# Encoder layer on one core: value projections computed token by token, a first stage without GpSimd arithmetic, merge transfers issued by GpSimd, scores two steps at a time

## The chip, the core and the metric

One core of a Trainium2 chip runs the whole program. The time is the device time of one execution in microseconds (us); less is better. Its engines each work through a queue of their own, in order: TensorE (PE; its weight loads are shown as PEld), VectorE (DVE), ScalarE (ACT), GpSimd (POOL), and SyncE (SP), which here only issues transfers. An instruction that waits holds up everything behind it in its engine's queue.

## The reference, cut to what matters

One layer of an encoder on 512 tokens of 1024 features, all float32:

```python
h = layer_norm(x, ln0_g, ln0_b)
proj = h @ w_in[l] + b_in[l]
y_a = (gate_b * dwconv3(gate_c * hin, conv_w[l])) @ w_a[l]
for g, (window, dil) in enumerate(((128, 1), (512, 4), (2048, 16))):
    o, lse = dilated_window_attention(q[:, :, g], k[:, :, g], v[:, :, g], dil, window // (2 * dil), slopes[g])
wts = jax.nn.softmax(jnp.stack(lses, 0), axis=0)
comb = jnp.sum(wts[..., None] * jnp.stack(outs, 0), axis=0)
mix = (g_a * y_a + g_b * (comb @ w_b[l])) @ w_o[l] + b_o[l]
h = layer_norm(ALPHA * h + mix, ln1_g[l], ln1_b[l])
f = gelu(dwconv3(a, ffn_conv_w[l]) + ffn_conv_b[l]) * gte      # a, gte: halves of h @ w_up + b_up
h = layer_norm(ALPHA * h + f @ w_down[l] + b_down[l], ln2_g[l], ln2_b[l])
```

There are three groups of 8 heads, 64 wide. The three groups' outputs of one head slot are added with weights that come from their softmax denominators: this is the "merge" below.

## The kernel before

**Number format.** Every matrix product is done three times with rounded operands: each operand is split into a high part and the rest (`hi` and `lo`), and `mm3` (L312) adds hi·hi, hi·lo and lo·hi. Weights come from memory as chunks of 128 x 2048 numbers (`load`, SP's queue), ACT copies the high part (L261) and DVE subtracts it from the raw chunk (L263). For the first two chunks POOL does the subtraction (`eng` in `split`). `raw`, `hi` and `lo` have rings of 2, 3 and 3 chunks.

**Units.** A unit is 128 columns of the input projection for all 512 tokens: 8 steps of the contraction, 24 products of 128x512, one half of a chunk. The result is feature-major (features on partitions). `in_units` lists them: for each of four head pairs p and each group g a q, a k and a v unit (36), then 24 for the convolution branch.

**First stage.** Token tiles x0 to x3 are loaded, normalised on DVE (L277 to L304), transposed on PE (L345), scaled on ACT and split into `hT` (`feature_major`, L308 to L310), first for x0 and x1 and then for x2 and x3. For each half of the tokens the first four units are computed with 256 columns. Forty products on zeros (`WARM`, L229) come ahead of it.

**Attention.** After each unit `slot` (L597) hands out a little attention work: `transpose_v` (L402) turns a v unit into token-major tiles (four PE transposes, an ACT copy, a DVE subtraction); `Job.a` computes scores of 128 or 256 queries and their exponentials (two jobs a slot for g = 0, one otherwise); `merge` (L525) sends the maxima and sums of group 0 through device memory to bring them into the order of groups 1 and 2 (L529 out, L533 in), computes the weights on DVE and ACT, and sends those of group 0 back (L550 out, L552 in). All four transfers are issued from ACT's queue. From three slots later `Job.b` (L474) scales the exponentials, `b2` (L479 to L482) transposes them, and `c` multiplies with the values; one job a slot each.

After attention follow the convolution's projection, the gates, the output projection, a layer norm, the MLP (L713 on) and the last layer norm.

The order on each engine is that of a scheduler, which starts from the program's order and moves instructions of one engine past each other; `keep_in_program_order` and `issue_after` bind it.

Of the kernel before, what the change touches and what calls it, by code (L numbers as in the profile page):

```python
# [11 lines left out]
P = 128  # L12
# [10 lines left out]
WARM = 40  # L23
# [24 lines left out]
def in_units():  # L48

    units = []  # L50
    for p in range(NPAIR):
        for g in range(3):
            for kind, base in (("q", BLK_Q), ("k", BLK_K), ("v", BLK_V)):
                units.append((kind, p, g, base + g * 4 + p))
    for j in range(8):
        units += [("C", j, 0, BLK_C + j), ("H", j, 0, BLK_H + j), ("B", j, 0, BLK_B + j)]
    return units


def chunk_plan():  # L60

    out = [("in", i, 2048) for i in range(0, len(in_units()), 2)]
# [16 lines left out]
def lay_out_weights(w):  # L79
# [10 lines left out]
    for name, key, cols in chunk_plan():  # L90
        if name == "in":
            c = [block(w_in, units[key + i][3] * P, P) for i in range(2)]
        elif name == "wa":
# [53 lines left out]
def build(tc, x, wst, colt, dist, rows, out):  # L147
# [3 lines left out]
    with ExitStack() as ctx:  # L151
        pool = lambda name, bufs=1, **k: ctx.enter_context(tc.tile_pool(name=name, bufs=bufs, **k))
        const = pool("const")
        wraw = pool("wraw", 2)
        whl = pool("whl", 3)
        blkp = pool("blk", 25)
# [43 lines left out]
        def first_raw(i, c):  # L200
            if i not in raws:
                raws[i] = wraw.tile([P, 2048], F32, tag="raw", name=f"raw{i}")
            src = wst[i * P * 2048 : (i + 1) * P * 2048].rearrange("(p c) -> p c", p=P)
            first_load(raws[i][:, c : c + 1024], src[:, c : c + 1024])
# [20 lines left out]
        for t in kbd:  # L225
            nc.vector.memset(f(t), 0.0)
# [14 lines left out]
        def load(i):  # L241
# [3 lines left out]
            t = wraw.tile([P, 2048], F32, tag="raw", name=f"raw{i}")  # L245
            src = wst[int(offs[i]) : int(offs[i + 1])].rearrange("(p c) -> p c", p=P)
            nc.sync.dma_start(out=t[:, :n], in_=src)
            raws[i] = t

        def split(i):  # L250
# [5 lines left out]
            lo = whl.tile([P, 2048], F32R, tag="lo", name=f"lo{i}")  # L256
            step = 512 if i == 0 else 1024
            starts = (0, 1024, 512, 1536) if i == 0 else range(0, n, step)
            for c in starts:
                part = slice(c, min(c + step, n))  # L260
                nc.scalar.activation(hi[:, part], raws[i][:, part], AF.Copy)  # L261
                eng = nc.gpsimd if i < 2 else nc.vector
                eng.tensor_tensor(lo[:, part], raws[i][:, part], f(hi[:, part]), op=ALU.subtract)  # L263
            splits[i] = (hi, lo)
# [10 lines left out]

        def bn_half(st, z, h):
            nc.vector.bn_stats(out=st[:, h, :], in_=z[:, h * 512 : (h + 1) * 512])  # L277
# [25 lines left out]
        def normalise(z, mean, rstd):  # L303
            nc.vector.tensor_scalar(z, z, mean, rstd, op0=ALU.subtract, op1=ALU.mult)  # L304

        def feature_major(pst, dst, kt, cg, cb, c0, c1):
            t = f32t("lnT")[:, : c1 - c0]
            nc.scalar.activation(t, pst, AF.Identity, bias=col(cb + kt), scale=col(cg + kt))  # L308
            nc.vector.tensor_copy(dst[:, 0, c0:c1], t)
            nc.vector.tensor_tensor(dst[:, 1, c0:c1], t, f(dst[:, 0, c0:c1]), op=ALU.subtract)  # L310
# [16 lines left out]
        first = []  # L327
        for hf in range(2):
# [5 lines left out]
            stats0 += ln_finish(st, f"l0{hf}")  # L334
            for r in rr:
                normalise(xt[r], *stats0[r])
            if hf == 0:
                with tc.issue_after(roots[0]):
                    chunk("in", 0)
            for k0 in range(0, KT, 2):  # L340
                pst = ps(("pt", "s")[k0 // 2 % 2])
# [4 lines left out]
                for k in (k0, k0 + 1):  # L346
                    c = (k % 2) * 256
                    feature_major(pst[:, c : c + 256], hT[k], k, C_G0, C_B0, hf * 256, hf * 256 + 256)
            if hf == 0:
                first = [ps("acc"), ps("acc"), ps("u"), ps("u")]  # L350
            t = slice(hf * 256, hf * 256 + 256)
            for n0, nk in ((0, [(n, k) for k in range(KT) for n in range(2)]), (2, [(n, k) for n in range(2) for k in range(KT)])):
                w = chunk("in", n0)
                for n, k in nk:
                    a = slice(n * 1024 + k * P, n * 1024 + (k + 1) * P)
                    mm3(first[n0 + n][:, t], w[0][:, a], w[1][:, a], hT[k][:, 0, t], hT[k][:, 1, t], k == 0, k == KT - 1)
# [55 lines left out]

        class Job:
# [6 lines left out]
            def a(self):  # L420
                p, g, n = self.key
                q = qk[p, g]
                if (p, g) not in sts:
                    sts[p, g] = small.tile([P, 2, 4, 2], F32, tag="st", name=f"st{p}{g}", bufs=8)
# [60 lines left out]
            def c(self):  # L485

                p, g, n = self.key
                v = vv[p, g]
# [11 lines left out]
                else:  # L500
                    for i in range(2):
                        j, cc = 2 * n + i, slice(i * 256, (i + 1) * 256)
                        mm3(u[:, cc], v[:, 0, j], v[:, 1, j], hi[:, cc], lo[:, cc], g == 1 and i == 0, g == 2 and i == 1)
# [21 lines left out]
        def merge(p):  # L525
# [7 lines left out]
            nc.scalar.dma_start(out=st0.rearrange("p a b c -> p (a b c)"), in_=s1.rearrange("(i r) s -> i (r s)", r=4))  # L533
# [16 lines left out]
            nc.scalar.dma_start(out=s2.rearrange("(i r) h -> i (r h)", r=4), in_=w[:, 7].rearrange("p a b -> p (a b)"))  # L550
            c0 = small.tile([P, 4, 2], F32, tag="c0", name=f"c0{p}", bufs=2)
            nc.scalar.dma_start(out=c0, in_=s2.rearrange("(b p) h -> p b h", p=P))  # L552
# [42 lines left out]
        wait = [0]  # L595

        def slot():  # L597
# [9 lines left out]
            if sums and sums[0].key[0] in cs and wait[0] == 0:  # L607
# [3 lines left out]
            if scores:  # L611
                for _ in range(2 if scores[0].key[1] == 0 else 1):
# [3 lines left out]
                if not any(x.key[0] == p for x in scores) and jb.key[1] == 2:  # L616
                    merge(p)
                    wait[0] = 3
                    order = [(0, 0), (0, 1), (0, 2), (0, 3), (1, 0), (2, 0), (1, 1), (2, 1)]
                    sums.extend(alljobs[(p,) + o] for o in order)  # L620
            wait[0] = max(0, wait[0] - 1)
            scores.extend(late)
            late.clear()

        alljobs = {}
        for n, (kind, a0, a1, blkno) in enumerate(in_units()):
# [6 lines left out]
            slot()  # L633
            if kind in "qkv":
# [7 lines left out]
            else:  # L642
                evac_conv(kind, a0, blkno, o)
# [202 lines left out]
```

## Time and profile before

| what | us |
|---|---|
| median of 3 runs | 988.76 |
| lowest and highest run | 987.72, 989.27 |
| the profiled execution | 988.83 |
| span from its first to its last instruction | 986.7 |
| busy in the span: PE, DVE, ACT, POOL | 968.7, 541.6, 398.2, 42.6 |

The profiled execution stands 0.07 us from the median; 2.1 us of it lie outside the span. Rows name an engine, a line of the kernel, an operation, its output and its inputs (buffer numbers left out), how many instructions the row joins, and their times. The end of a matmul in these rows is modelled, so that neighbouring matmuls overlap in them and "busy" is not the rate of PE; the rate is read from how many start in a stretch.

### The profile page before, as it was taken

What the parts mean: (1) busy time and instruction counts of PE and PEld (TensorE: products, weight loads), DVE (VectorE), ACT (ScalarE), POOL (GpSimd) and SP (SyncE); (2) the same over time, 40 slices, a digit from 0 to 9 for tenths busy, and PEclk for the clock granted to TensorE, in tenths of its full rate; (3) what the DMA queues carried; (4) which work ended last, traced back from release to release, by engine and by line L of the source; (5) the groups of instructions that cost most, each with busy time, mean ns of one, the idle gap of its engine ahead of it and who ended that gap; (6) DMA issues with size and microseconds to landing.
All of it is one profiled execution on the core that took longest, in us unless ns stands there. A gap on an engine that the chain in (4) does not pass through costs nothing.

```text
span 986.7 us, 11756 instructions
## 1 busy us (share of the span) xinstructions
PE 968.7 (98%) x4729; PEld 817.0 (83%) x4729; DVE 541.6 (55%) x874; ACT 398.2 (40%) x679; POOL 42.6 (4%) x150
## 2 busy tenths in 40 slices
PE   7999999999999999999999999999999999999996
PEld 6988888888888888888888888988888888888885
DVE  7856757568565554421344757668443254454256
ACT  4655555555543333322343324544441134443220
POOL 4000000000000000000000000010000000000000
PEclk8999999999999999999999999999999999999998
DMA  6322321222222222225234321242322323222402
GB/s 232 129 87 86 87 86 44 86 86 86 44 86 86 86 86 86 86 86 205 93 107 133 122 88 43 102 176 86 128 75 75 128 88 126 86 86 84 151 4 83
DMA packets 23462, 96.74 MB, mean 98 GB/s; under 512 B 9200, under 2 KB 9584, under 8 KB 13680
## 3 DMA queue, kind: packets, MB, share of 16 engines
q1 hardware_dynamic: 14256, 89.60, 26.1%
q0 software_dynamic: 1728, 6.29, 1.9%
q10 hardware_dynamic: 7424, 0.10, 0.4%
q8 instruction: 37, 0.61, 0.3%
q14 instruction: 17, 0.14, 0.0%
HBM read 93.84 MB, written 2.15 MB: 97 GB/s over the span
## 4 chain that ended last, share of the span: by engine, by line
PE 91%; DVE 4%; DMA 2%; ACT 2%; issue 0%; ACTq 0%; DVEq 0%
PE ps_acc L313 15%; PE ps_acc L314 15%; PE ps_acc L315 15%; PE ps_u L313 5%; PE ps_u L314 5%; PE ps_u L315 5%; PE ps_s L313 5%; PE ps_s L314 5%; PE ps_s L315 5%; PE ps_pt L313 4%; PE ps_pt L315 4%; PE ps_pt L314 4%; DMA s<-st 1%; PE ps_pt L479 1%; ACT hi L261 1%; DVE kbd L392 1%
## 5 line engine op out<-in xcount | busy, mean ns | idle before, releaser
L263 DVE TENSOR_TENSOR lo<-raw,hi 128x1024 fp32r<-128x1024 f32 (+1 forms) x160 | 190.7, 1211 | 186.7 <-ACT hi L261 185.3
L261 ACT ACTIVATE hi<-raw 128x1024 fp32r<-128x1024 f32 (+1 forms) x166 | 166.6, 1033 | 232.9 <-PE ps_acc L314 67.6
L313 PE MATMUL ps_acc<-hT,hi 128*128 128x512 f32 (+1 forms) x512 | 198.5, 388 | 2.0 <-DVE kbd L392 1.7
L314 PE MATMUL ps_acc<-hT,hi 128*128 128x512 f32 (+1 forms) x512 | 196.9, 385 | 0.0
L315 PE MATMUL ps_acc<-hT,lo 128*128 128x512 f32 (+1 forms) x512 | 196.7, 384 | 0.0
L313 PEld LDWEIGHTS ps_acc<-hT,hi 128*128 128x128 f32 x512 | 96.6, 189 | 21.1 <-issue 1.5
L315 PEld LDWEIGHTS ps_acc<-hT,lo 128*128 128x128 f32 x512 | 96.6, 189 | 19.3
L314 PEld LDWEIGHTS ps_acc<-hT,hi 128*128 128x128 f32 x512 | 96.8, 189 | 17.8 <-DVE hT L310 0.2
L460 ACT ACTIVATE S<-S,nm 128x128 f32<-128x128 f32 (+2 forms) x96 | 40.1, 419 | 54.2 <-DVE nm L458 47.5
L566 DVE SCALAR_TENSOR_TENSOR cv<-fp,cols,cv 128x512 f32<-128x512 f32 x22 | 16.5, 751 | 64.5 <-ACT cv L565 64.5
L314 PE MATMUL ps_acc<-h1T,hi 128*128 128x512 f32 (+1 forms) x96 | 36.0, 375 | 0.0
L313 PE MATMUL ps_acc<-h1T,hi 128*128 128x512 f32 (+1 forms) x96 | 35.8, 373 | 0.0
L313 PE MATMUL ps_pt<-h1T,hi 128*128 128x512 f32 (+1 forms) x96 | 35.6, 371 | 0.0
L314 PE MATMUL ps_pt<-h1T,hi 128*128 128x512 f32 (+1 forms) x96 | 35.6, 371 | 0.0
L315 PE MATMUL ps_pt<-h1T,lo 128*128 128x512 f32 (+1 forms) x96 | 35.6, 371 | 0.0
L313 PE MATMUL ps_u<-h1T,hi 128*128 128x512 f32 (+1 forms) x96 | 35.6, 371 | 0.0
L314 PE MATMUL ps_u<-h1T,hi 128*128 128x512 f32 (+1 forms) x96 | 35.6, 371 | 0.0
L315 PE MATMUL ps_u<-h1T,lo 128*128 128x512 f32 (+1 forms) x96 | 35.6, 371 | 0.0
L314 PE MATMUL ps_s<-h1T,hi 128*128 128x512 f32 (+1 forms) x96 | 35.6, 371 | 0.0
L313 PE MATMUL ps_s<-h1T,hi 128*128 128x512 f32 (+1 forms) x96 | 35.6, 371 | 0.0
L315 PE MATMUL ps_s<-h1T,lo 128*128 128x512 f32 (+1 forms) x96 | 35.6, 371 | 0.0
L315 PE MATMUL ps_acc<-h1T,lo 128*128 128x512 f32 (+1 forms) x96 | 35.6, 371 | 0.0
(369 smaller groups left out, 1902.8 us busy)
## 6 DMA issues: line engine op xcount, KB each, us to landing
raw<-wst SPq DMA_DIRECT2D x76, 1024.0 KB, 4.8
raw<-wst SPq DMA_DIRECT2D x4, 768.0 KB, 4.3
x<-x SPq DMA_DIRECT2D x4, 512.0 KB, 6.5
raw<-wst SPq DMA_DIRECT2D x4, 512.0 KB, 8.5
hb<-x POOLq DMA_DIRECT2D x4, 512.0 KB, 4.3
out<-hb SPq DMA_DIRECT2D x7, 256.0 KB, 2.1
ln_g<-rows POOLq DMA_DIRECT2D x3, 512.0 KB, 4.4
ln_b<-rows POOLq DMA_DIRECT2D x3, 512.0 KB, 5.9
```

The costliest lines, as they stand in the source:

```text
L261: nc.scalar.activation(hi[:, part], raws[i][:, part], AF.Copy)
L263: eng.tensor_tensor(lo[:, part], raws[i][:, part], f(hi[:, part]), op=ALU.subtract)
L313: nc.tensor.matmul(o, ah, bh, start=start, stop=False)
L314: nc.tensor.matmul(o, ah, bl, start=False, stop=False)
L315: nc.tensor.matmul(o, al, bh, start=False, stop=stop)
L392: nc.vector.scalar_tensor_tensor(lo, src, bb, f(hi), op0=ALU.add, op1=ALU.subtract)
L460: nc.scalar.activation(v, v, AF.Exp, bias=nm[:, j : j + 1], scale=0.125, accum_out=dn[:, j : j + 1])
L479: nc.tensor.transpose(pt[:, j * P : (j + 1) * P], self.pe[:, j * P : (j + 1) * P], ident)
L566: nc.vector.scalar_tensor_tensor(a, u[:, 128:640], col(c + step), a, op0=ALU.mult, op1=ALU.add)
```

## The change

- **Values token by token.** For groups 1 and 2 the v units go. In their place a product with the tokens' `hT` as the stationary operand and 512 weight columns as the moving one gives the values of all four pairs for 128 tokens: `values`, 4 times 24 products of 128x512 for each group, after the units of chunks 4 and 6. `evac_values` adds the bias (a row, broadcast by a transfer on GpSimd's queue) and splits. No transposes are needed for these groups.
- **First stage.** The `lo` of the first two chunks is computed by DVE at fixed places; the two `kbd` memsets go to POOL; DVE's order is pinned; four casts of the first half move to ACT (L352); products and their order are listed by hand; 56 warm-up products instead of 40.
- **Rings.** `raw` is 3 halves of a chunk (before: 2 chunks), `lo` 5 halves (before: 3 chunks), and the first two chunks live in the general pool, which grows from 25 to 28 tiles.
- **Merge.** Its four transfers per pair are issued from POOL's queue, and the first one's rows are 16 bytes and not 8.
- **Slots.** Scores are issued two jobs a slot for all groups; the countdown of three slots is kept per pair; an extra slot without new scores follows each v unit after the first.

```diff
-WARM = 40
+WARM = 56
...
+                if kind != "v" or g == 0:
+                    units.append((kind, p, g, base + g * 4 + p))
...
+V_AFTER = {4: 1, 6: 2}
...
+        if i in V_AFTER:
+            out += [("vt", (V_AFTER[i], kh), 2048) for kh in range(2)]
...
-        wraw = pool("wraw", 2)
+        wraw = pool("wraw", 3)
         whl = pool("whl", 3)
-        blkp = pool("blk", 25)
+        blkp = pool("blk", 28)
...
-            nc.vector.memset(f(t), 0.0)
+            nc.gpsimd.memset(f(t), 0.0)
...
+            for c in range(0, n, 1024):
+                t = wraw.tile([P, 1024], F32, tag="raw", name=f"raw{i}")
+                nc.sync.dma_start(out=t[:, : min(1024, n - c)], in_=src[:, c : min(c + 1024, n)])
...
+                los = [whl.tile([P, 1024], F32R, tag="lo", name=f"lo{i}", bufs=5) for _ in range(0, n, 1024)]
...
-                eng = nc.gpsimd if i < 2 else nc.vector
-                eng.tensor_tensor(lo[:, part], raws[i][:, part], f(hi[:, part]), op=ALU.subtract)
+                if i > 1:
+                    low(i, hi, Pieces(los), part)
...
+        def pin(ins):
+            return tc.keep_in_program_order(ins) if pinned[0] else ins
...
+            if cast:
+                nc.scalar.activation(dst[:, 0, c0:c1], pst, AF.Identity, bias=col(cb + kt), scale=col(cg + kt))
...
+            if hf == 1:
+                for n in range(2):
+                    low(1, *splits[1], slice(n * 1024, n * 1024 + 1024))
...
+                if hf == 0 and k0 % 4 == 0:
+                    for n in range(2):
+                        low(0, *splits[0], slice(n * 1024 + k0 * P, n * 1024 + (k0 + 4) * P))
...
+        first_norm(0)
+        with tc.issue_after(roots[0]):
+            chunk("in", 0)
+        first_features(0)
+        first = [ps("acc"), ps("acc"), ps("u"), ps("u")]
+        first_products(0, 0, halves)
+        first_norm(1)
+        first_products(0, 2, two[:-8])
+        last = first_features(1)
...
+        vbias = blk(F32, (2, 512), "vbias")
+        nc.gpsimd.dma_start(out=vbias.rearrange("p a b -> p (a b)"), in_=vrow.partition_broadcast(P))
...
+        def values(g, j, ws):
+            o = ps("acc")
+            ts = slice(j * P, (j + 1) * P)
+            for k in range(KT):
+                w, b = ws[k // 4], slice(k % 4 * 512, k % 4 * 512 + 512)
+                mm3(o, hT[k][:, 0, ts], hT[k][:, 1, ts], w[0][:, b], w[1][:, b], k == 0, k == KT - 1)
+            return o
...
+        def evac_values(g, j, o):
+            a = f32t("vsum")
+            nc.vector.tensor_tensor(a, o, vbias[:, g - 1], op=ALU.add)
+            t = blk(F32R, (2, 4, P), f"vt{g}{j}")
+            nc.scalar.activation(t[:, 0], a.rearrange("p (a b) -> p a b", a=4), AF.Copy)
+            nc.vector.tensor_tensor(t[:, 1], a.rearrange("p (a b) -> p a b", a=4), f(t[:, 0]), op=ALU.subtract)
...
-            nc.scalar.dma_start(
-                out=s1.rearrange("(b p) (s h) -> p s b h", p=P, h=2), in_=sts[p, 0]
-            )
+            nc.gpsimd.dma_start(out=s1.rearrange("(b p) c -> p b c", p=P), in_=sts[p, 0].rearrange("p s b h -> p b s h"))
...
-            nc.scalar.dma_start(out=c0, in_=s2.rearrange("(b p) h -> p b h", p=P))
+            nc.gpsimd.dma_start(out=c0, in_=s2.rearrange("(b p) h -> p b h", p=P))
...
-            if scores:
-                for _ in range(2 if scores[0].key[1] == 0 else 1):
+            if scores and new:
+                for _ in range(2):
...
+            if kind == "v" and a0 > 0:
+                slot(False)
...
+            if n - 1 in V_AFTER:
+                g = V_AFTER[n - 1]
+                ws = [chunk("vt", (g, kh)) for kh in range(2)]
+                for j in range(4):
+                    o = values(g, j, ws)
+                    slot()
+                    evac_values(g, j, o)
```

Three places show how instructions move. First DVE at the beginning of the program, from the normalising of x0 on; `hT` are the split features, `lo0` the rest of the first weight chunk. Before:

```order
L304 TENSOR_SCALAR x0_80<-x0_80,l00mv_161 128x1024
L304 TENSOR_SCALAR x1_81<-x1_81,l00mv_161 128x1024
L226 MEMSET kbd0_102 128x1024
L226 MEMSET kbd1_103 128x1024
L309 CAST hT0_147<-lnT_196 128x256
```

and changed:

```order
L346 TENSOR_SCALAR x0_80<-x0_80,l00mv_179 128x1024
L346 TENSOR_SCALAR x1_81<-x1_81,l00mv_179 128x1024
L298 TENSOR_TENSOR lo0_192<-raw0_86,hi0_191 128x512
L298 TENSOR_TENSOR lo0_193<-raw0_89,hi0_191 128x512
L354 CAST hT0_165<-lnT_214 128x256
```

Two memsets have gone from before the first cast, and two subtractions for the first weight chunk stand there; two more follow behind the features of step 3.

Second, the merge of pair 2. Before, on ACT (`s12` and `st02` are the transfers out and in of group 0's maxima and sums, `cb0` the finished output of pair 0):

```order
L460 ACTIVATE S_1643,st20_1567<-S_1643,nm_1650 128x192 x2
L529 DMA s12_2029<-st20_1567 256x4x2
L409 ACTIVATE v21_1733<-ps_pt_1728 128x512
L533 DMA st02_2031<-s12_2029 128x16
L521 ACTIVATE cb0_1744<-cm_1165 128x512
L481 ACTIVATE PT_1752<-ps_pt_1747 128x512
```

and changed, on POOL:

```order
L564 MEMSET S_1851 128x2x64
L630 DMA s12_2136<-st20_1764 128x4x4
L632 DMA st02_2138<-s12_2136 128x16
L564 MEMSET S_2287 128x2x64
L657 MEMSET up0_2680 128x1
L658 MEMSET up0_2680 128x1
L649 DMA s22_2156<-mrg2_2140 128x8
L651 DMA c02_2158<-s22_2156 128x4x2
```

The transfers have left ACT's queue; behind the one that waits stand memsets on POOL now, and no activation.

Third, DVE where pair 1's weights come back (`c01`; `mrg1` are the weights that need no transfer). Before:

```order
L474 TENSOR_TENSOR S_1177<-S_1177,mrg1_1451 128x512
L482 TENSOR_TENSOR PT_1521<-ps_pt_1516,PT_1521 128x512
L474 TENSOR_TENSOR S_1370<-S_1370,mrg1_1451 128x512
L474 TENSOR_TENSOR S_1247<-S_1247,mrg1_1451 128x512
L474 TENSOR_TENSOR S_1431<-S_1431,mrg1_1451 128x512
L474 TENSOR_TENSOR S_999<-S_999,c01_1469 128x512
```

and changed:

```order
L575 TENSOR_TENSOR S_1501<-S_1501,mrg1_1667 128x512
L575 TENSOR_TENSOR S_1630<-S_1630,mrg1_1667 128x512
L575 TENSOR_TENSOR S_1518<-S_1518,mrg1_1667 128x512
L575 TENSOR_TENSOR S_1647<-S_1647,mrg1_1667 128x512
L298 TENSOR_TENSOR lo15_1913<-raw15_1800,hi15_1912 128x1024
L488 TENSOR_TENSOR v20_1760<-ps_pt_1755,v20_1760 128x512
L575 TENSOR_TENSOR S_1304<-S_1304,c01_1685 128x512
```

Six instructions stand between the last weights and the first use of `c01`, where there were five, one of them longer.

## Rows read from the trace of the kernel before

**Rows 1.** The page: busy time by engine, and the chain that ended last.
```profile
PE 968.7 (98%) x4729; PEld 817.0 (83%) x4729; DVE 541.6 (55%) x874; ACT 398.2 (40%) x679; POOL 42.6 (4%) x150
...
PE 91%; DVE 4%; DMA 2%; ACT 2%; issue 0%; ACTq 0%; DVEq 0%
```

**Rows 2.** Windows: stretch, length, busy us and instructions by engine, PE clock, DMA share, GB/s.
```profile
7.00:12.00 5.00, 0.28 (x3) 0.00 (x0) 4.60 (x11) 2.58 (x5) 3.08 (x3) 0.93 1.00 398
12.00:18.00 6.00, 5.43 (x24) 5.03 (x25) 5.68 (x13) 3.38 (x8) 2.76 (x2) 0.50 0.83 300
18.00:28.70 10.70, 10.70 (x90) 10.70 (x90) 10.47 (x24) 4.47 (x6) 5.54 (x4) 0.99 0.37 132
...
160.00:205.00 45.00, 43.86 (x220) 36.16 (x219) 29.51 (x55) 22.70 (x55) 0.21 (x1) 1.00 0.22 70
...
255.00:285.00 30.00, 28.55 (x157) 24.44 (x156) 16.60 (x30) 15.92 (x41) 0.14 (x2) 1.00 0.31 74
...
700.00:800.00 100.00, 100.00 (x443) 82.81 (x442) 37.28 (x43) 29.35 (x36) 2.63 (x16) 1.00 0.28 100
```

**Rows 3.** The chain of waits, where a v unit is transposed: start us, us, what.
```profile
62.49 0.44 PE ps_pt L406 x4
```

**Rows 4.** Timeline of PE in the first stage: start us, us, instructions [idle before <-releaser].
```profile
16.16 0.78 PE L313 MATMUL ps_acc<-hT,hi 128*128 128x256 f32 x2
...
43.03 0.66 PE L406 MATMUL ps_pt<-cols,vT 128*128 128x128 f32 x4 [0.63 <-ACT vT L397]
```

**Rows 5.** Timeline of DVE, and of POOL, in the first stage.
```profile
9.04 1.15 DVE L294 TENSOR_TENSOR l00mv<-l00mv 128x2 f32<-128x2 f32 x1
10.23 3.40 DVE L304 TENSOR_SCALAR x<-x,l00mv 128x1024 f32<-128x1024 f32 x2
...
15.70 0.42 DVE L309 CAST hT<-lnT 128x256 fp32r<-128x256 f32 x2
...
19.93 1.27 DVE L277 BATCH_NORM_STATS2 l02st<-x 128x6 f32<-128x512 f32 x2
...
22.67 2.30 DVE L289 TENSOR_SCALAR l01mv<-l01mv 128x2 f32<-128x2 f32 x1
...
25.63 0.16 DVE L294 TENSOR_TENSOR l01mv<-l01mv 128x2 f32<-128x2 f32 x1
25.82 1.53 DVE L304 TENSOR_SCALAR x<-x,l01mv 128x1024 f32<-128x1024 f32 x2
...
8.91 5.85 POOL L263 TENSOR_TENSOR lo<-raw,hi 128x512 fp32r<-128x512 f32 x4 [8.47 <-ACT hi L261]
```

**Rows 6.** Timeline of ACT in the first stage.
```profile
16.44 1.03 ACT L308 ACTIVATE lnT<-ps_pt,cols 128x256 f32<-128x256 f32 x2
...
18.23 2.04 ACT L261 ACTIVATE hi<-raw 128x1024 fp32r<-128x1024 f32 x2
```

**Rows 7.** Timeline of ACT around two merges.
```profile
182.12 0.62 ACTq L529 DMA_DIRECT2D s<-st  x1
...
190.36 0.63 ACT L521 ACTIVATE cb<-cm 128x512 fp32r<-128x512 f32 x1 [5.66 <-DMA s<-st]
...
261.69 0.63 ACT L521 ACTIVATE cb<-cm 128x512 fp32r<-128x512 f32 x1 [6.70 <-DMA s<-st]
```

**Rows 8.** DMA issues: count, KB each, median us to landing.
```profile
s<-mrg ACTq DMA_DIRECT2D x4, 4.0 KB, 1.4
c<-s ACTq DMA_DIRECT2D x4, 4.0 KB, 1.9
```

**Rows 9.** Timeline of DVE around pair 1's weights, of POOL issuing a transfer.
```profile
161.49 1.89 DVE L474 TENSOR_TENSOR S<-S,mrg 128x512 f32<-128x512 f32 x3
165.90 1.90 DVE L474 TENSOR_TENSOR S<-S,c 128x512 f32<-128x512 f32 x3 [2.52 <-DMA c<-s]
167.71 1.22 DVE L263 TENSOR_TENSOR lo<-raw,hi 128x1024 fp32r<-128x1024 f32 x1
...
512.05 0.53 POOL L701 DMA_DIRECT2D hb<-x  x1 [49.88 <-DVE gate L689]
```

More of the change, by code (lines that the diff above doesn't have):

```diff
@@ L326, in build, with first_norm @@
         hT = [blk(F32R, (2, 512), f"hT{k}") for k in range(KT)]
-        first = []
-        for hf in range(2):
+        def first_norm(hf):
             rr = (2 * hf, 2 * hf + 1)
@@ L347, in build, with first_products @@
                     c = (k % 2) * 256
-                    feature_major(pst[:, c : c + 256], hT[k], k, C_G0, C_B0, hf * 256, hf * 256 + 256)
-            if hf == 0:
-                first = [ps("acc"), ps("acc"), ps("u"), ps("u")]
+                    last = feature_major(pst[:, c : c + 256], hT[k], k, C_G0, C_B0, hf * 256, hf * 256 + 256, hf == 0 and k >= 4)
+            return last
+        def first_products(hf, n0, steps):
+            w = splits[n0 // 2]
             t = slice(hf * 256, hf * 256 + 256)
[L352 to L356, printed above, removed]
+            for n, k, m in steps:
+                a = slice(n % 2 * 1024 + k * P, n % 2 * 1024 + (k + 1) * P)
+                wk, hk = w[m // 2][:, a], hT[k][:, m % 2, t]
+                nc.tensor.matmul(first[n][:, t], wk, hk, start=k == 0 and m == 0, stop=k == KT - 1 and m == 2)
+        halves = []
+        for ks in (range(0, 4), range(4, 8)):
+            halves += [(n, k, m) for k in ks for n in range(2) for m in range(2)]
+            halves += [(n, k, 2) for k in ks for n in range(2)]
+        two = [(n, k, m) for n in (2, 3) for k in range(KT) for m in range(2)]
+        two += [(n, k, 2) for n in (2, 3) for k in range(KT)]
+        whole = [[(n, k, m) for k in range(KT) for m in range(3)] for n in range(4)]
+        first_norm(0)
[7 more added lines that the diff above has]
+        last = first_features(1)
+        first_products(0, 2, two[-8:])
+        with tc.issue_after(last):
+            chunk("in", 2)
+        first_products(1, 0, [(n, k, m) for k in range(KT) for n in range(2) for m in range(3)])
+        for n in range(2, 4):
+            first_products(1, n, whole[n])
+        pinned[0] = False
         def evac_split(o, bias, hi, lo, src):
@@ L593, in build, with slot @@
         vtodo, late, scores, sums, scaled, running = [], [], [], [], [], []
-        wait = [0]
-        def slot():
+        wait, ready = [0], {}
+        def slot(new=True):
             while vtodo:
@@ L606, in slot @@
                 running.append(jb)
-            if sums and sums[0].key[0] in cs and wait[0] == 0:
+            if sums and ready[sums[0].key[0]] <= wait[0]:
                 jb = sums.pop(0)
@@ L617, in slot @@
                     merge(p)
-                    wait[0] = 3
+                    ready[p] = wait[0] + 3
                     order = [(0, 0), (0, 1), (0, 2), (0, 3), (1, 0), (2, 0), (1, 1), (2, 1)]
                     sums.extend(alljobs[(p,) + o] for o in order)
-            wait[0] = max(0, wait[0] - 1)
-            scores.extend(late)
-            late.clear()
+            wait[0] += 1
+            if new:
+                scores.extend(late)
+                late.clear()
         alljobs = {}
```

78 lines of the change are left out of this document (51 added, 27 removed).

## The prediction

> **What bounds the kernel now.** I read the page's engine line and chain first. PE is busy for 968.7 of 986.7 us and makes up 91% of the chain that ended last [rows 1]: the time goes down only where PE has less to do or waits less. Since the ends of matmuls are modelled, I take PE's pace from starts. In the MLP 443 products of 512 columns start in 100 us, one every 0.226 us; in the first stage 90 of 256 columns start in 10.7 us, one every 0.119 us, at a clock of 0.99 [rows 2]. The reader should then look in the windows for stretches in which PE is not full. [...] Attention loses 45.00 - 43.86 = 1.14 us from 160 to 205 us and 30.00 - 28.55 = 1.45 us from 255 to 285 us [rows 2]. From 285 us to the end of the MLP nothing is idle, so there only removed PE work counts.
>
> **Transposes that go.** Of twelve v units eight lose their transposes. A set of four takes 0.44 us on the chain [rows 3]: 8 x 0.44 = 3.5 us off PE, which is the bound there, so all of it comes back. The products themselves do not change: eight units of 24 products of 512 columns become eight of the same, at the same 0.226 us. On ACT a copy out of PSUM and a cast become one cast; on DVE an addition (about the 0.63 us of rows 9 for 128x512) joins the subtraction: 8 x 0.63 = 5 us, spread over eight units of 24 x 0.226 = 5.4 us each, in which DVE otherwise has a chunk half (1.22 us) and two score steps to do. I cost that at nothing; without that cover it would be 0.6 us a unit.
>
> **The first stage.** Before, POOL subtracts the first weight chunk while DVE normalises, and the rows show what that costs DVE: L294 takes 1.15 us beside POOL and 0.16 us without, a pair of L304 3.40 against 1.53, and one 128x2 instruction (L289) 2.30 us, some 2.1 more than L294's kind needs [rows 5]. Step by step:
>
> - x1 is normalised at 10.23 + 3.40 = 13.63 us before. Without POOL this is 0.99 + 1.87 = 2.86 us earlier, 10.8 us. Against that stands a transfer that the change adds at the start: the bias rows, 128 x 4 KB, on POOL's queue behind the two memsets. The DMA engines are full at 398 GB/s just then [rows 2], so 512 KB cost the loads of x and weights 0 to 1.3 us; I take 0.7, the middle, since the two queues share: 11.5 us.
> - The two `lo` parts that now stand ahead of the first cast take half of 1.22 us each [rows 9]: the first cast at 12.7 us instead of 15.70, the first product about 0.46 us behind it as before (16.16) [rows 4, 5], 13.2 us. So PE starts 3 us earlier, and sixteen more warm-up products shorten the hole ahead of it.
> - But PE does not finish 3 us earlier. ACT now does twelve activations for these features (before: eight) at 1.03/2 us, with both parts of the second chunk (2.04 us) among them [rows 6]: 12 x 0.52 + 2.0 = 8.2 us from about 12, so 20.2 us, and DVE, whose order is pinned, ends the half at 20.5 us. Before, it went on to x2 and x3 at 19.93 [rows 5].
> - From there to both normalised it took 25.82 + 1.53 - 19.93 = 7.4 us; less the 2.1 of L289, plus two `lo` parts of 1.22 that now stand ahead, it takes 7.7: 28.2 us. PE has its first-half work done by then (192/2 x 0.119 = 11.4 us from 13.2, held up by the features until 20.5 and by the `lo` parts to about 26).
> - Then 12 transposes of 0.11 us and 96 x 0.119 = 11.4 us: 41.0 us. Before, the next work started at 43.03, after 0.63 us of waiting for ACT [rows 4]; the new order has one chunk part instead of two on ACT ahead of that evacuation, so I let the wait go. **Gain 2.0 us.** If PE were never held up, 13.2 - 0.7 + 192 x 0.119 + 28 x 0.11 = 38.4 and the gain 4.6 us; if the transfer costs its full 1.3 us and a hole before the second half halves the clock for some 2 us of work, it is 0.
>
> **Merges.** ACT holds back its queue while L533 waits for the transfer ahead of it: 5.66 us at 190 and 6.70 us at 261 us [rows 7]. Behind it stand a `cb` copy, a `PT` copy and a q evacuation, and PE waits for these through DVE; the two idle stretches lie right there. On POOL the same wait holds up memsets that are needed several units later. Of 1.14 + 1.45 = 2.6 us I take 2.4 back. What is late next is DVE: `c01` is awaited there (2.52 us before [rows 9]). Between the last weights and that wait DVE now has four scalings, a `lo` part and a subtraction, 5 x 0.63 + 1.22 = 4.4 us of work, and the way out and back took 1.4 + 1.9 = 3.3 us [rows 8]. No row shows these transfers on POOL's queue. The nearest is `hb`, 0.53 us of POOL for 128 rows [rows 9]; `c` has 512 rows, so between 0.5 and 2.1 us, and the way becomes 4 to 6 us: a wait of 0 to 1.6 us on DVE per pair, while PE still has a unit of 5.4 us in hand. I cost it at nothing and keep 4 x 1.6 = 6 us as the far bound. [...] That DVE and POOL shut each other out, the rows of L304 show (1.7 us each beside POOL, 0.8 without [rows 5]); that DVE holds up a transfer of POOL's queue, none shows.
>
> **Slots and rings.** Two score steps a slot move DVE work together. From 160 to 205 us DVE is busy 29.5 of 45 us [rows 2]; with seven units a pair instead of nine its share rises to about 0.66 x 9/7 = 0.85 at most. It stays below 1, so I cost it at nothing; a late evacuation is what would show. The `lo` ring of five halves makes DVE wait for PE to release a half, but a half is released a whole unit (5.4 us) before its successor's product and takes 1.2 us: nothing. SP's issues double in number at the same bytes: nothing.
>
> **Sum.** 3.5 + 2.0 + 2.4 = 7.9 us. The span goes from 986.7 to 978.8 us, with the 2.1 us outside it 980.9; from the median, 0.07 us away, 988.8 - 7.9 = **980.9 us**.
>
> **Rivals.**
>
> - *Transfers come late on POOL's queue.* For: 512 short rows of `c`, and that DVE and POOL do shut each other out [rows 5]. Against: DVE has 4.4 us of cover, PE 5.4 more. The 2.4 us do not come back and half of the 6 us reach PE: 7.9 - 2.4 - 3 = 2.5 us gained, 986.3 us. [...]
> - *The idle in attention was never ACT's.* If DVE's bursts hold PE up, two score steps a slot do so again and this part of the change does not do what it says: 5.5 us gained, 983.3. For: DVE's 0.85. Against: both idle stretches follow ACT's two waits.
> - *PE never waits in the first stage:* 4.6 instead of 2.0, 978.3 us. Against: twelve activations and two chunk parts on one engine.
> - *Slower: DVE stands still at `c`.* Everything that PE needs next (scores, q evacuation, chunk parts) is behind the scaling that waits there, four times. It costs PE what the way out and back exceeds 4.4 + 5.4 = 9.8 us by, and the gain is gone at 9.8 + 7.9/4 = 11.8 us. One transfer did take 190.36 - 182.12 = 8.2 us in the trace, behind a weight load [rows 7]; if both of a pair's do, 16.4 us, this is 4 x 6.6 = 26 us lost, 26.4 - 7.9 = 18 us slower, 1007 us. The medians of 1.4 and 1.9 us speak against it.
>
> **How the numbers follow.** A change of 0.2% (2 us) is about what a measurement of this kernel can tell from none. Chances: the forecast (979 to 983 us) 0.57; idle of DVE's making 0.15; PE never waiting 0.12; late transfers 0.11; DVE standing still 0.05. The range is 977.5 to 985.5 us: the best first stage with all idle gone at the low end, no first-stage gain and a third of the late transfers' cost at the high end; outside it lie the standstill, the worse part of the late transfers and a rest, 0.15 to 0.2. Faster by over 2 us covers all cases but the standstill and the edge of the late transfers: 0.92; within 2 us 0.04; slower 0.04.
>
> **What would show it.** Right: 208 PE transposes of 128x128 instead of 240; L346 at 0.8 us each; first product near 13 us, the first v transposes near 41 us; no idle on ACT that ends with a DMA; PE full to within 1 us from 160 us on. Wrong: a wait of DVE's scaling for `c` of several us, a granted clock of 0.5 around 28 us, or evacuations that keep `ps_acc` full while PE is idle.

## The result and the profile after

The changed kernel takes 983.07 us (median of 4 runs, 983.05 to 983.32) against 988.92 us (4 runs): the ratio is 0.9945 with a 95% interval of 0.9932 to 0.9957. Forecast were 980.9 us, 977.5 to 985.5. The sign and the range held; of 7.9 us that were expected, 5.85 came.

The page of the changed kernel: busy time by engine and the chain that ended last, beside [rows 1].

```profile
PE 964.7 (98%) x4713; PEld 813.5 (83%) x4713; DVE 551.1 (56%) x882; ACT 395.9 (40%) x675; POOL 55.3 (6%) x163
...
PE 92%; DVE 3%; ACT 2%; DMA 2%; issue 1%; SPq 0%; DVEq 0%; ACTq 0%; POOLq 0%
```

PE bounds it as before. Where did the time go? Two moments that both kernels have cut the span in three: the first transposes of a v unit (the first stage is over) and the first transposes of the second layer norm's output. These are PE's rows at the second moment, the first of the kernel before, the second of the changed one; the first moment is in [rows 4] and in the timeline further down.

```profile
608.07 0.38 PE L733 MATMUL ps_u<-cols,hb 128*128 128x128 f32 x2
```

```profile
602.58 0.38 PE L842 MATMUL ps_u<-cols,hb 128*128 128x128 f32 x2
```

| | before | changed | gain |
|---|---|---|---|
| start to the first v transposes | 43.03 | 41.81 | 1.22 |
| from there to the `hb` transposes | 565.04 | 560.77 | 4.27 |
| from there to the end of the span | 378.63 | 378.72 | -0.09 |
| profiled time less span | 2.13 | 1.77 | 0.36 |

The middle stretch holds the 32 transposes that went, 32 x 0.109 = 3.5 us. Only 0.8 us are left for PE's waits, where the merges alone were to give 2.4. The windows of the changed kernel show why (columns as in [rows 2]):

```profile
100.00:160.00 60.00, 59.56 (x302) 50.46 (x302) 39.01 (x70) 31.15 (x61) 3.24 (x7) 1.00 0.27 81
160.00:205.00 45.00, 44.19 (x215) 36.46 (x215) 34.76 (x75) 26.45 (x69) 2.46 (x5) 1.00 0.21 70
205.00:255.00 50.00, 48.39 (x264) 41.66 (x263) 38.64 (x83) 29.82 (x74) 2.17 (x7) 1.00 0.23 75
255.00:285.00 30.00, 30.00 (x168) 26.12 (x167) 18.50 (x39) 18.48 (x54) 2.98 (x6) 1.00 0.22 72
```

The stretch from 255 to 285 us is full now. But 0.44, 0.81 and 1.61 us stand idle in the others. Idle time did not go; it moved. PE's list of waits from 45 to 320 us names what it waits for (releaser, us in total, times, longest):

```profile
PE ps_u L358 <- ACT PT L582: 2.1, 2, 1.6
PE ps_acc L358 <- DVE kbd L470: 0.6, 1, 0.6
PE ps_s L358 <- DVE nm L559: 0.2, 1, 0.2
```

The longest is this one: PE, then ACT, in the timeline around 231 us.

```profile
229.50 1.03 PE L580 MATMUL ps_pt<-cols,S 128*128 128x128 f32 x8
230.27 0.19 PEld L358 LDWEIGHTS ps_acc<-hT,hi 128*128 128x128 f32 x1
...
230.61 0.40 PE L359 MATMUL ps_acc<-hT,hi 128*128 128x512 f32 x1
...
230.96 1.04 ACT L474 ACTIVATE vT<-ps_acc,cols 128x448 f32<-128x448 f32 x1
...
231.96 1.08 ACT L582 ACTIVATE PT<-ps_pt 128x512 fp32r<-128x512 f32 x2
...
232.62 0.39 PE L358 MATMUL ps_u<-PT,vt 128*128 128x256 f32 x1 [1.61 <-ACT PT L582]
```

Eight transposes stand in a row, two sets of attention weights. Two products later PE wants `PT`, the copy of what it has just transposed, and ACT still has the v evacuation (L474, the copy of the v unit out of PSUM) ahead of it. In program order two slots lie side by side here: the normal one and the extra one that the change puts behind each v unit of pairs 1 to 3. A set of weights that the first slot transposes is multiplied by the second, with no unit between them.

The first stage, on PE and DVE:

```profile
13.21 1.86 PE L408 MATMUL ps_acc<-hT,hi 128*128 128x256 f32 x10 [0.91 <-DVE hT L354]
16.19 0.39 PE L408 MATMUL ps_u<-hT,hi 128*128 128x256 f32 x1 [1.11 <-ACT hi L292]
...
24.69 2.08 PE L408 MATMUL ps_u<-hT,lo 128*128 128x256 f32 x16
27.87 0.30 PE L396 MATMUL ps_pt<-cols,x 128*128 128x128 f32 x1 [1.11 <-DVE x L346]
...
30.04 0.51 PE L408 MATMUL ps_acc<-hT,hi 128*128 128x256 f32 x2
...
41.81 0.64 PE L484 MATMUL ps_pt<-cols,vT 128*128 128x128 f32 x4
```

```profile
9.18 1.53 DVE L346 TENSOR_SCALAR x<-x,l00mv 128x1024 f32<-128x1024 f32 x2
...
11.89 0.69 DVE L298 TENSOR_TENSOR lo<-raw,hi 128x512 fp32r<-128x512 f32 x1 [0.58 <-ACT hi L292]
12.87 0.29 DVE L354 CAST hT<-lnT 128x256 fp32r<-128x256 f32 x1 [0.28 <-ACT lnT L350]
...
20.64 1.28 DVE L319 BATCH_NORM_STATS2 l02st<-x 128x6 f32<-128x512 f32 x2
...
26.91 1.53 DVE L346 TENSOR_SCALAR x<-x,l01mv 128x1024 f32<-128x1024 f32 x2
```

Without POOL beside it, a pair of L346 takes 1.53 us in both halves ([rows 5]: 3.40 and 1.53). The first product starts 2.95 us earlier than in [rows 4]; of that, PE keeps 1.22, since it now waits for x2 and x3.

These two executions do not stand at one clock, though. In the kernel before, the granted clock is 0.50 of full speed until about 18.1 us; it fell at about 11.3 us, while PE waited 4.73 us for x0. From its first product on PE waits for nothing until 42.4 us, so that it pays in full for what the clock takes:

```profile
16.00:18.00 2.00, 2.00 (x11) 2.00 (x10) 2.00 (x9) 2.00 (x6) 0.00 (x0) 0.50 0.84 299
```

Nine starts from 16.16 to 18.20 us take 2.04 us there and not 9 x 0.119 = 1.07. The changed kernel's first stage ran at 1.00 throughout. So about 1.0 of the 1.22 us is the clock's in these two executions (an estimate from these rows), and 0.2 us would be left at one clock.

The new transfers (KB, median us to landing; POOL's queue):

```profile
vbias<-vrow POOLq DMA_DIRECT2D x1, 512.0 KB, 8.1
...
s<-mrg POOLq DMA_DIRECT2D x4, 4.0 KB, 1.7
c<-s POOLq DMA_DIRECT2D x4, 4.0 KB, 2.7
```

### The profile page after: what moved, and what is told of

The parts are those of the page before. It is cut to its first block, busy times and chain, and to the rows that moved or that the text cites. A ratio compares the mean times of both kernels' runs of the same rounds, so it can differ in the third digit from the quotient of the medians.

```text
span 981.3 us, 11983 instructions
## 1 busy us (share of the span) xinstructions
PE 964.7 (98%) x4713; PEld 813.5 (83%) x4713; DVE 551.1 (56%) x882; ACT 395.9 (40%) x675; POOL 55.3 (6%) x163
## 4 chain that ended last, share of the span: by engine, by line
PE 92%; DVE 3%; ACT 2%; DMA 2%; issue 1%; SPq 0%; DVEq 0%; ACTq 0%; POOLq 0%
PE ps_acc L358 15%; PE ps_acc L360 15%; PE ps_acc L359 15%; PE ps_u L358 5%; PE ps_s L360 5%; PE ps_s L358 5%; PE ps_s L359 5%; PE ps_u L360 5%; PE ps_u L359 5%; PE ps_pt L360 4%; PE ps_pt L358 4%; PE ps_pt L359 4%; PE ps_pt L580 1%; DMA raw<-wst 1%; PE ps_acc L408 1%
## 5 line engine op out<-in xcount | busy, mean ns | idle before, releaser
L298 DVE TENSOR_TENSOR lo<-raw,hi 128x1024 fp32r<-128x1024 f32 (+1 forms) x166 | 198.3, 1199 | 236.4 <-ACT hi L292 102.0
L358 PE MATMUL ps_acc<-hT,hi 128*128 128x512 f32 x416 | 164.3, 395 | 0.6 <-DVE kbd L470 0.6
L360 PE MATMUL ps_acc<-hT,lo 128*128 128x512 f32 x416 | 162.3, 390 | 0.0
L359 PE MATMUL ps_acc<-hT,hi 128*128 128x512 f32 x416 | 162.0, 390 | 0.0
L360 PEld LDWEIGHTS ps_acc<-hT,lo 128*128 128x128 f32 x416 | 78.1, 188 | 16.7
L358 PEld LDWEIGHTS ps_acc<-hT,hi 128*128 128x128 f32 x416 | 78.2, 188 | 16.5 <-PE ps_pt L580 0.8
L359 PEld LDWEIGHTS ps_acc<-hT,hi 128*128 128x128 f32 x416 | 78.2, 188 | 15.5
L659 POOL COPY fp<-fp 128x127 f32<-128x127 f32 x22 | 14.0, 635 | 318.0 <-ACT fp L885 318.0
```

Of the source, the lines that this page charges most:

```text
L298: ins = nc.vector.tensor_tensor(lo[:, part], Pieces(raws[i])[:, part], f(hi[:, part]), op=ALU.subtract)
L358: nc.tensor.matmul(o, ah, bh, start=start, stop=False)
L359: nc.tensor.matmul(o, ah, bl, start=False, stop=False)
L360: nc.tensor.matmul(o, al, bh, start=False, stop=stop)
L659: nc.gpsimd.tensor_copy(u[:, 1:128], u[:, 512:639])
```

## The experiments

Each experiment ran beside the kernel before on the same chip, which took 988.3 to 989.0 us there; a difference below that 0.7 us between two experiments says little by the time alone. "v" is the start of the first v transposes in the profiled execution, "middle" the time from there to the `hb` transposes: the first tells of the first stage alone, the second of attention and what follows. The mean granted clock from 45 to 285 us was 1.00 in every row but e3 (see 2).

| run | us | v | middle |
|---|---|---|---|
| before | 988.92 | 43.03 | 565.04 |
| changed | 983.07 | 41.81 | 560.77 |
| e1_before_pool | 985.15 | 43.64 | 562.54 |
| e2_after_act | 983.19 | 42.01 | 560.07 |
| e3_after_one | 983.04 | 42.99 | 560.87 |
| e4_after_act_one | 982.04 | 42.02 | 559.28 |
| e5_no_extra_slot | 980.56 | 42.33 | 558.12 |
| e6_extra_mid | 981.06 | 43.34 | 559.14 |
| e7_vbias_last | 982.70 | 40.56 | 561.81 |
| e8_hi1_last | 980.59 | 39.41 | 560.78 |
| e9_two_edits | 978.03 | 39.38 | 558.15 |
| e10_three_edits | 978.00 | 38.62 | 559.06 |
| e11_dummy_T | 986.93 | 41.90 | 564.54 |
| e12_warm40 | 983.24 | 41.81 | 560.63 |

**1. Were ACT's waits the idle time of the kernel before?** In the kernel before, this line and the three others like it:

```diff
-            nc.scalar.dma_start(out=c0, in_=s2.rearrange("(b p) h -> p b h", p=P))
+            nc.gpsimd.dma_start(out=c0, in_=s2.rearrange("(b p) h -> p b h", p=P))
```

> The kernel before with nothing changed but the four merge transfers of a pair, which POOL's queue issues and not ACT's. Theory A (ACT's waits for these transfers made PE idle around 191 and 265 us, and POOL's queue brings it back): about 2.4 us less than before, 986.5 us, and no idle time on ACT that ends with a transfer. Theory B (that idle time has another cause, ACT's waits were hidden): within 0.5 us of before, 988.9, with the same two idle stretches on PE. Theory C (transfers come late on POOL's queue): slower than before by up to 6 us, with a long wait of DVE's scaling for c.

Measured: 985.15 us, ratio 0.997 (0.9958 to 0.9982), and the middle stretch is 565.04 - 562.54 = 2.50 us shorter. PE's waits from 45 to 320 us, the two that count in the kernel before, and all of this run:

```profile
PE ps_acc L313 <- DVE kbd L392: 1.7, 2, 1.3
PE ps_u L314 <- DVE PT L482: 0.5, 1, 0.5
```

```profile
PE ps_s L313 <- DVE S L453: 0.7, 1, 0.7
PE ps_s L313 <- DVE nm L458: 0.2, 1, 0.2
PE ps_acc L313 <- DVE kbd L392: 0.2, 1, 0.2
```

The waits around 191 and 265 us are gone, and theory A holds. By the starts of the same products in both traces, 3.2 us come back there and 0.8 us are lost at 171 us, where the scores wait for DVE; DVE stood 3.42 us for `c` just before (2.52 in the kernel before [rows 9]). That the net is as large as the 2.4 us of the prediction is in part luck, since the prediction had no such loss in it.

**2. Is it worth anything in the changed kernel, and what do two score steps a slot cost?** Three kernels: the change with its four transfers back on ACT (the diff above, turned round), with one score step a slot for groups 1 and 2, and with both.

```diff
-                for _ in range(2):
+                for _ in range(2 if scores[0].key[1] == 0 else 1):
```

> The changed kernel with its merge transfers back on ACT's queue, rows of 16 bytes as in the change. Theory A: ACT's waits come back and the idle time of PE grows by about 2.4 us, 985.5 us. Theory B: no change, 983.1 us within 0.5. Theory C: some tenths faster than the change.

> The changed kernel with one score step a slot for groups 1 and 2, as before the change (two for group 0). Theory A1 (the 4.0 us that PE still waits in attention come from bursts of two steps on DVE and ACT): 2 to 3.5 us less, 979.5 to 981 us, and the 1.8 us stretch at 231 us is gone. Theory A2 (they come from products with the values that stand too close behind the transposes of the weights, whatever the scores do): within 0.7 us of the change, 983.1, with such stretches at other places.

> The changed kernel with both undone: transfers on ACT's queue and one score step a slot for groups 1 and 2; values token by token, the first stage and the rings stay. Theory A with A1: 2.4 us above the run with one step a slot, about 982.5. Theory B: equal to that run. What is then left between this run and the kernel before (988.9) is worth the values and the first stage: 4.7 us by the trace of the change (3.5 and 1.2), so 984.2 us if attention waits as it did before.

Measured: 983.19, 983.04 and 982.04 us. On the changed kernel the transfers on ACT are no slower: its middle stretch is even 0.7 us shorter than with POOL, the time the same. So theory A, right for the kernel before, does not carry over to the new order: there ACT waits 5.0 us for the way out of pair 1's weights, and PE's list of waits is the same as in the changed kernel but for its last line.

The run with one step a slot (e3) needs care. Its profiled execution was the slowest of four (981.41 to 984.35 us), and the clock fell in it behind PE's longest wait (2.21 us). The first row is this run, the second the same work in the run with both edits (e4), whose products start 1.57 us closer together there:

```profile
230.00:234.00 4.00, 3.59 (x13) 3.31 (x14) 3.34 (x11) 3.11 (x6) 0.00 (x0) 0.57 0.37 131
```

```profile
229.00:233.00 4.00, 3.56 (x20) 3.16 (x21) 3.33 (x11) 3.10 (x6) 0.00 (x0) 1.00 0.40 131
```

Less these 1.57 us its middle stretch is about 559.3 us (an estimate), as in e4 (559.28). Of the two answers to what PE waits for, A1 does not hold as it was put: with one step a slot the 0.6 us for `kbd` go, but the wait for `PT` grows to 2.2 us in both runs, and 2 to 3.5 us do not come. The second step is not free either. With the transfers on ACT, at a clock of 1.00 in both runs, one step shortens the middle stretch by 560.07 - 559.28 = 0.8 us and the time by 1.15 us; on POOL's queue it is 560.77 - 559.3 = 1.5 us by the estimate.

What POOL's queue adds shows in DVE's timeline of the changed kernel and of e2, and in POOL's of the changed kernel:

```profile
186.06 0.69 DVE L488 TENSOR_TENSOR v<-ps_pt,v 128x512 fp32r<-128x512 f32 x1
189.93 0.69 DVE L575 TENSOR_TENSOR S<-S,c 128x512 f32<-128x512 f32 x1 [3.17 <-DMA c<-s]
```

```profile
187.64 1.22 DVE L298 TENSOR_TENSOR lo<-raw,hi 128x1024 fp32r<-128x1024 f32 x1 [3.05 <-ACT hi L292]
...
189.50 0.68 DVE L575 TENSOR_TENSOR S<-S,c 128x512 f32<-128x512 f32 x1
```

```profile
182.09 0.56 POOL L649 DMA_DIRECT2D s<-mrg  x1 [28.21 <-DVE mrg L647]
186.73 0.75 POOL L651 DMA_DIRECT2D c<-s  x1 [4.09 <-DMA s<-mrg]
```

The way out takes 4.64 us at pair 1 (with ACT's queue 4.06 at the same place) and the way back some 3 more, so DVE stands for 3.17 us. With the transfers on ACT it does not wait for `c`, but it stands for 3.05 us one step earlier, behind ACT's `hi`, which comes after ACT's own wait for that transfer. What POOL's queue costs DVE is the rest: the first scaling by `c` starts at 189.93 and not at 189.50, in a run whose v transposes came 0.2 us earlier, so 0.6 us. PE's 0.7 us follow right behind it: the score products at 192.4 us start 0.45 us later than in e2, the next unit's at 193.4 another 0.18.

**3. The extra slot.** Left out, or put into the middle of the v unit's 24 products:

```diff
-            if kind == "v" and a0 > 0:
-                slot(False)
```

```diff
             for k in range(n):
+                if between and k == n // 2:
+                    between()
...
+                extra = kind == "v" and a0 > 0
+                unit(o, w, (n % 2) * 1024, hT, between=(lambda: slot(False)) if extra else None)
```

> The changed kernel without the extra slot behind the v units of the later pairs. In the changed kernel's trace PE waits 0.62, 0.23 and 1.78 us at 126, 178 and 231 us, each time where that slot puts two slots side by side, so that the products with a set of weights stand right behind the transposes of the same weights and wait for the copy on ACT. Theory X (this is the new wait that took what the transfers gave): these three go, attention's idle time on PE falls by about 2.4 us and the time to 980.7 us. Theory Y (ACT's queue is too full there, whatever the slots do): the idle time turns up at neighbouring products, and the time stays within 0.7 of 983.1 us.

> The changed kernel with the extra slot in the middle of the v unit's products instead of right behind the other slot. Theory X: as without the extra slot, 2.4 us less, 980.7 us, since half a unit (2.7 us) now stands between the transposes and the products. Theory Y: within 0.7 us of 983.1.

Measured: 980.56 and 981.06 us; the middle stretch is 2.65 and 1.63 us shorter. Theory X holds: in both the waits at 126 and 231 us are gone. The run with the slot in the middle is the purer test, since the other short waits stay there (0.71 us for `kbd` at 201 us among them) and it pays some 0.6 us at new places. Leaving the slot out does more: the countdown of three slots then spans more units, and DVE's waits for `c` fall from 3.9 to 0.3 us. The other short waits of PE go too, the 0.23 us at 178 us among them, and PE's list of waits has one line left, at 286 us, where a unit of the convolution waits for ACT:

```profile
PE ps_acc L358 <- ACT Csb L676: 1.5, 1, 1.5
```

**4. What holds up the first stage?** The bias rows behind the first loads (SP's queue); and the second chunk's high parts behind the twelve activations (`acts[-1]` is the last L352 of the first half):

```diff
-        nc.gpsimd.dma_start(out=vbias.rearrange("p a b -> p (a b)"), in_=vrow.partition_broadcast(P))
+        first_load(vbias.rearrange("p a b -> p (a b)"), vrow.partition_broadcast(P))
```

```diff
         with tc.issue_after(roots[0]):
-            chunk("in", 0)
+            split(0)
+        load(2)
         first_features(0)
+        with tc.issue_after(acts[-1]):
+            split(1)
```

> The changed kernel with the transfer of the bias rows on SP's queue, behind the loads of the first stage, instead of at the start on POOL's. In the changed kernel the loads from the second half of the first chunk on land 1.28 us later than before. Theory V (that is passed on in full, since the first products wait for the second half of the first chunk and ACT for the second chunk): first product at 12.0 us instead of 13.2, first transposes of v at 40.6 instead of 41.8, 981.9 us. Theory W (ACT's chain of twelve activations and the order pinned on DVE set the end of the stage, not the loads): first product earlier, v transposes within 0.4 us of 41.8, 983.1 us.

> The changed kernel with the high parts of the second chunk behind the twelve activations on ACT's queue and not among them. Theory W: the features of the first half are done 2.0 us earlier (18.4 us instead of 20.4), x2 and x3 are normalised at about 26.5 us instead of 28.4, PE does not wait at 27 us, first transposes of v at 40 to 40.5 us and 981.3 to 981.8 us. Theory V: the loads set the pace, so the features wait for other things and the v transposes stay within 0.4 us of 41.8; if PE wants the second chunk earlier than ACT now has it, up to 1 us slower.

Measured: 982.70 us with v at 40.56, and 980.59 us with v at 39.41. Both holds are there. The late bias rows bring the end of the stage 1.25 us forward, as theory V said, but the total by only 0.4: the middle stretch grows by 1.0 us. ACT now takes a weight part (34.94 us in its timeline) ahead of the first units' copies, and DVE's last `kbd` subtraction ends no earlier than in the changed kernel:

```profile
40.76 1.16 DVE L470 SCALAR_TENSOR_TENSOR kbd<-ps_acc,cols,kbd 64x512 fp32r<-64x512 f32 x1
```

```profile
39.51 2.36 DVE L470 SCALAR_TENSOR_TENSOR kbd<-ps_acc,cols,kbd 64x512 fp32r<-64x512 f32 x2 [1.07 <-ACT kbd L468]
```

That is 41.92 us in e7 (the first row) and 41.87 us in the changed kernel (the second); PE's list has 0.7 us for it in e7 and nothing in the changed kernel. The high parts are the larger hold. PE's order follows that edit: the products with the second chunk, which stand among those with the first in the changed kernel (16.19 us), come behind them. In e8's timeline ACT has copied all features at 17.9 us instead of 20.3, and the parts follow:

```profile
17.24 0.62 ACT L352 ACTIVATE hT<-ps_s,cols 128x256 fp32r<-128x256 f32 x1
17.69 3.97 ACT L292 ACTIVATE hi<-raw 128x1024 fp32r<-128x1024 f32 x4
```

In the changed kernel the last feature, the two parts that stood among them, and ahead of these the second half of the first chunk, for which ACT waits 2 us:

```profile
11.23 1.15 ACT L292 ACTIVATE hi<-raw 128x512 fp32r<-128x512 f32 x2 [2.04 <-DMA raw<-wst]
...
15.08 1.06 ACT L292 ACTIVATE hi<-raw 128x1024 fp32r<-128x1024 f32 x1 [0.42 <-DMA raw<-wst]
...
16.94 1.05 ACT L292 ACTIVATE hi<-raw 128x1024 fp32r<-128x1024 f32 x1
...
19.68 0.59 ACT L352 ACTIVATE hT<-ps_s,cols 128x256 fp32r<-128x256 f32 x1
```

**5. Together.** No extra slot and the high parts later; then the bias rows later as well.

> The changed kernel without the extra slot and with the second chunk's high parts behind the twelve activations. If the two holds are separate, their gains add: 983.1 - 2.5 - 2.5 = 978.1 us, first transposes of v at 39.4 us, attention's idle time on PE about 2.8 us. If the earlier start only moves attention into new waits, 979.5 us or more.

> As the run with the two edits, and the bias rows behind the first loads on SP's queue. Theory V: the loads from the second half of the first chunk on come 1.28 us earlier and the first stage ends up to 1.2 us earlier, 977.0 us. Theory W: as in the run with that edit alone, the end of the stage is then given back at the evacuation of the first units, 0.3 us or less gained, 977.8 to 978.1 us.

Measured: 978.03 (977.84 to 978.10) and 978.00 us, ratio 0.9892 (0.9877 to 0.9907) and 0.9891. The two gains add to a tenth of a microsecond; the third edit is given back as before (v 0.8 us earlier, the middle 0.9 longer). The kernel with two edits beats the changed one by 5.0 us.

**6. The transposes and the warm-up alone.** Thirty-two transposes that nobody reads, and `WARM = 40`.

```diff
                     evac_values(g, j, o)
+                    pv = ps("pt")
+                    for i in range(4):
+                        nc.tensor.transpose(pv[:, i * P : (i + 1) * P], vbias[:, 0, i * P : (i + 1) * P], ident)
```

> The changed kernel with four transposes of 128x128 added behind each of the eight evacuations of values, of the bias rows into a PSUM tile that nobody reads: the 32 transposes that the change took off PE, without the work of ACT and DVE that went with them. If each costs PE its full pitch, 32 x 0.1095 = 3.5 us, 986.6 us. If PE's waits in attention (5.5 us in the changed kernel) take some of them up, 985 to 986 us.

> The changed kernel with 40 warm-up products, as before the change. The hole ahead of the first transposes grows from 1.3 to about 3 us; these transposes start when DVE has normalised x0, at 10.0 us in either case. If a longer hole brings the clock of 0.5 that the kernel before shows from 12 to 18 us, the first stage ends later by about the 1.2 us by which it did in the run with one step a slot (granted clock 0.5 from 17 to 21 us), 984.3 us. If the clock stays at 1.0, no change, 983.1 us.

Measured: 986.93 us (10 runs, 985.39 to 988.27), 3.9 above the changed kernel, with 3.77 in the middle stretch: each transpose costs PE its full pitch (3.77 / 32 = 0.118 us, where from one start to the next it is 0.109), and its waits take up none of it (by the starts of products, a set of four costs 0.36 to 0.49 us where it stands, and nothing comes back later). With 40 warm-up products it is 983.24 us, v at 41.81 to the hundredth: the sixteen that were added are worth nothing. The granted clock did fall for a while in that run (0.85 from 9 to 13 us, 0.73 from 13 to 17), but it was back before PE's next wait, for `hi` ahead of 16.17 us, and that wait took the loss up (0.63 us in place of 1.11).

## Why the prediction came out as it did

- **Transposes, 3.5 us: right.** 32 fewer, at 0.109 us; the run that puts them back measures 3.8 to 3.9. DVE's additions are free as costed: PE waits for `vsum` or `vt` nowhere.
- **First stage, 2.0 us: 1.2, of which the clock is about 1.0 by estimate.** The first product was forecast at 13.2 us and came at 13.21; the first half's end on DVE at 20.5 and came at 20.73; x2 and x3 at 28.2 and came at 28.44; the wait of 0.63 us at the end went as said. The size was off in the last line of that sum. It counted 12 transposes of 0.11 us, where there are 16 (two tiles by eight features) with two short stops, 30.04 - 27.87 = 2.2 us instead of 1.3, and the 96 products took 11.8 instead of 11.4. What it did not price is the clock of the kernel before, 0.50 from 12 to 18 us [rows 2]: about 1.0 us of the 43.03 us that it set its sum against. Both profiled executions of that order (before, e1) fell to 0.50 there; of the twelve of the changed kernel and its variants seven kept 1.00 through the stage. Whether the change brought that about, no run shows. Inside the sum a second size was off: the bias rows delay the loads by 1.2 us and not 0.7 (the second half of the first chunk, x2 and x3 land at 11.21, 12.49 and 13.77 us, before at 9.98, 11.27 and 12.55), about what 512 KB take at the 411 GB/s of that stretch (1.28 us, an estimate). That the two queues share made it no less: the bias rows landed at 10.57 us, between loads that landed at 7.46 and 11.21, and the three loads named, which came after, were late by 1.22 to 1.23 us each. The first product fell on 13.2 us all the same: x1, whose load comes ahead, was normalised at 9.18 + 1.53 = 10.7 us and not at 11.5.
- **Merges, 2.4 us: the mechanism right, the sum wrong.** Put on the kernel before, POOL's queue gives 2.5 us in the middle stretch (3.2 come back, 0.8 are lost). In the changed kernel the net of all waits there is 0.8, or 0.5 with the transposes at e11's 3.77 us. The step that failed is the paragraph "Slots and rings", which put two score steps a slot at nothing and left the extra slot out. The second step costs 0.8 us (e4 against e2), and 1.5 by the estimate for e3. The extra slot puts `c` of a job right behind its `b2`, and the order on PE has eight transposes in a row there; 0.62 and 1.78 us of waiting follow at the v units of pairs 1 and 3 (from the starts of neighbouring products, less their pitch). Moving the slot gives 1.6 us back, leaving it out 2.65.
- **"What is late next is DVE": right, and cheaper than its bound.** DVE does wait 3.17 us for `c`, above the 1.6 that the text allowed, since the way out at pair 1 took 4.64 us and not 1.4. That is no matter of POOL: ACT's queue needs 4.06 there, and in the kernel before it took 4.4 us at the same pair, which the median of 1.4 hides. Elsewhere the way out and back is 105.99 - 104.03 + 2.7 = 4.7 us against 3.3 [rows 8]. Of the 1.4 us between them POOL's longer issuing is part (0.56 and 0.75 us a transfer, against 0.33 and 0.38 on ACT's queue in the kernel before). PE pays 0.7 us for POOL's queue in the changed kernel (e2) and 0.8 in the kernel before (e1); with one step a slot, at one clock, nothing shows (e3, e4).
- **The rivals.** The second one's number, 983.3 us, was met by luck: the idle time was ACT's, as e1 shows. Its reason holds for the 0.8 us that the second score step costs (1.5 by the estimate); the extra slot, which it did not have, is worth more. The first came true in a small way, 0.7 us. The other two did not come.
- **What was to show it.** 208 transposes, L346 at 0.8 us and the first product were as said. "PE full to within 1 us from 160 us on" was the sign that failed: 0.81 + 1.61 us. "No idle on ACT that ends with a DMA" held for the merges, but from 45 to 310 us ACT now waits 8.8 us for weight loads. And of the signs of a wrong prediction one came, DVE's wait for `c`.

What stays open: the 0.36 us outside the span, how much of the first stage's gain would be left at one clock (0.2 us is an estimate), and why the wait at 286 us appears when the extra slot goes (1.5 us, also in the best version). No run here tells.

## What to carry to other kernels

When work is dealt out in slots, ask of every added slot what now stands next to what: a producer's last step on one engine and its consumer on another need other work between them; here half a unit (2.7 us, e6) was enough. The order of the instructions shows what stands next to what. A wait that a change removes is worth what the new order still had to pay for it; test the removal on the old kernel and on the new one, since here it gave 2.5 us on the one, while on the other its time is the same as without it and its middle stretch 0.7 us longer. And a transfer that is needed late should not be issued early: here it took about its full time (1.2 us) from the loads queued behind it. Last, look at the granted clock of both executions before their stretches are compared: in two places here it stood for 1.0 and 1.57 us.

## What the runs showed of the hardware

The same first stage took up to 1.5 us more in some executions, and a lower granted clock goes with it. These are the same two microseconds of the changed kernel and of e3, whose instructions up to there are the same, at a granted clock of 1.00 and of 0.50:

```profile
17.00:19.00 2.00, 2.00 (x19) 2.00 (x18) 0.57 (x2) 2.00 (x5) 0.00 (x0) 1.00 1.03 412
```

```profile
17.00:19.00 2.00, 2.00 (x11) 2.00 (x11) 0.58 (x2) 2.00 (x5) 0.00 (x0) 0.50 1.03 412
```

In both PE had waited about 1 us at 12 and 1.1 us at 15 us. In e3 the first half's products ended 2.7 us later and v came at 42.99 instead of 41.81 us; e6 shows the same (43.34, at 0.50 from 17 to 21 us). At 230 us the clock of e3 fell once more, behind 2.21 us of waiting; e4 waited as long at the same place and kept 1.00. So one profile of this stage can mislead by more than some of the edits are worth; the middle stretch was compared apart from it for that reason.
